# Row sums of an attention kernel: block transposes on VectorE instead of a transpose on TensorE, and a later turn for the last pair's first half

## The chip, the cores and the metric

The kernel runs on one core of one Trainium2 chip. The metric is the device time of one execution in microseconds; lower is better. The engines are called PE (TensorE; PEld is its weight load), DVE (VectorE), ACT (ScalarE), POOL (GpSimd) and SP (SyncE, which here only issues DMAs).

## The reference

Two encoder layers over 1024 tokens of width 1024, in float32. Layer 0 mixes with neighbourhood attention (mixer A), layer 1 with grouped-query attention (mixer B); both have 16 query heads of 64 dims, a softmax, and a gate. Cut to what matters here:

```python
sc = jnp.einsum('bkgqd,bksd->bkgqs', qb, k).astype(jnp.float32) * scale
pr = jax.nn.softmax(sc, axis=-1).astype(v.dtype)
o  = jnp.einsum('bkgqs,bksd->bkgqd', pr, v)
...
return (o * jax.nn.silu(gate)) @ w_out
```

After each mixer come a residual add, a second gated addition (per-layer embedding) and, at the end, one RMS norm.

## The kernel before

**Staging.** Mixer A, a dense stage, mixer B, a second dense stage. Matmuls work on float32 split in a high and a low part, so most products take three matmuls (L300 is the one line through which all of them go).

**Attention.** For each head and query tile: S (scores, with a row minimum `mn` by VectorE), E (exponential by ScalarE, with row sums `rs`), T (P transposed by PE into PSUM, then split by ScalarE into `PTh` and by VectorE into `PTl`), AV (PTh and PTl times V, into the PSUM tile `o`, four query tiles side by side). In mixer A all transposes, P's and others, draw on a PSUM pool of two buffers named `t`; in mixer B the pool of `o` has one buffer.

**The end of a head.** When the AV of half a head's queries is complete, `head_end` puts down what has to follow. Two heads (a pair) and one half of the queries (`hf`) share the tiles `Y` (outputs, 64 rows of each head), `rb` and `r8` (128 x 8: inverse row sums of four query tiles of the two heads). `evac` (L478) copies one half of `o` to Y, `join` (L441) adds the other half, which frees `o`; `norm` (L468) takes the reciprocal of the row sums. The outputs lie with queries along the free dimension, the inverse sums with queries along the partitions, so the sums have to be turned:

- For pairs 0 to 6, `rows` transposes `r8` on PE into PSUM (L445), ScalarE copies the 8 rows out (L447), SP stores them to DRAM as `rD` (L449), and two loads on SP bring them back to `rb`, each row of 512 values broadcast to 64 partitions (L451).
- For pair 7 `spread` (L455) copies the sums out along the free dimension and `across` (L461) transposes four 128 x 128 tiles on PE. For `hf` 0 ScalarE copies the result to `rb` (L464), for `hf` 1 it is used from PSUM.

`fin` then multiplies Y by the gate and by `rb` on POOL (L512, L513), and later ScalarE and VectorE split it (L509, L510) and SP stores it. `fin_last` does the same for pair 7 on VectorE; it calls `across` itself if that has not come yet.

**The order.** Every engine runs its instructions in the order in which the code emits them, and that order is written by hand. A list of attention items (one S, E, T or AV each) is mixed with dense items (projections and gates) by their costs. After each attention item comes one pulse. `post.add(n, f)` calls f n pulses later; `later` counts query tiles in the same way. So `evac` comes `DO` pulses after the last AV, `join` one pulse after it, `rows` `DD[layer][0]` pulses after the reciprocal, the store and the loads `DD[layer][1]` pulses after `rows`, and `across` `DT` pulses after the reciprocal. In mixer B two AV items lie nine or more pulses apart. Where one engine has to wait, all that stands behind in its queue waits too.

There are 28 groups that go through `rows`: 7 pairs, 2 halves, 2 layers. Four go through `across`.

Of the kernel before, what the change touches and what calls it, by code (L numbers as in the profile page):

```python
# [11 lines left out]
F32 = mybir.dt.float32  # L12
# [3 lines left out]
AF = mybir.ActivationFunctionType  # L16
# [16 lines left out]
DG, DR, DQ, DY, NP = 1, 2, 2, 1, 8  # L33
KT, KN = 2, 4
DO = (2, 3)
DD = ((3, 2), (5, 2))
DT = 2
FIN = (4, 4)
HOLD = 2
DP = 1  # L40
# [112 lines left out]
def trunk(ctx, tc, x, wts, rpb, gains, hgains, mask, rope, out):  # L153
    nc = tc.nc
    sync, act, dve, pool, pe = nc.sync, nc.scalar, nc.vector, nc.gpsimd, nc.tensor
# [7 lines left out]
    ident = glob.tile([128, 128], F32, name="ident")  # L163
# [133 lines left out]
    post = Later()  # L297
# [131 lines left out]
    def head_end(sb, h, hf, rs, Ops, ylive, layer, gg, talloc):  # L429
        pair = h // 2  # L430
        b = (h % 2) * 64
        if h % 2 == 0:
            Y = sb.tile([128, 512], F32, name="Y", bufs=2)
            rb = sb.tile([128, 512], F32, name="rb", bufs=2)
            r8 = sb.tile([128, 8], F32, name="r8", bufs=4)
            ylive[pair, hf] = (Y, rb, r8, {})
        Y, rb, r8, tail = ylive[pair, hf]
        yh = Y[b:b + 64]

        def join():  # L440
            dve.scalar_tensor_tensor(yh, Ops[0:64], 0.5, yh, op0=ALU.mult, op1=ALU.add)  # L441

        def rows():
            ps = talloc()
            pe.transpose(ps[0:8, 0], r8, ident)  # L445
            r8T = sb.tile([8, 128], F32, name="r8T", bufs=2)
            act.activation(r8T, ps[0:8, 0], AF.Copy)  # L447
            rD = dram.tile([8, 128], F32, name="rD", bufs=4)
            post.add(DD[layer][1], lambda: sync.dma_start(rD, r8T))  # L449
            for i in range(2):  # L450
                post.add(DD[layer][1], lambda i=i: sync.dma_start(  # L451
                    rb[64 * i:64 * i + 64], bass.AP(tensor=rD.tensor, offset=rD.offset + 512 * i, ap=[[0, 64], [1, 512]])))

        def spread():
            dve.tensor_copy(rb.rearrange("p (t j c) -> p t j c", t=4, j=2),  # L455
                            r8.rearrange("p (j t) -> p t j", j=2)[:, :, :, None].to_broadcast([128, 4, 2, 64]))

        def across():
            ps = talloc()
            for t in range(4):  # L460
                pe.transpose(ps[:, t], rb[:, t * 128:(t + 1) * 128], ident)  # L461
            ps = ps.rearrange("p t c -> p (t c)")
            if hf == 0:
                act.activation(rb, ps, AF.Copy)  # L464
            tail["rb"] = rb if hf == 0 else ps

        def norm():
            dve.reciprocal(r8[:, 4 * (h % 2):4 * (h % 2) + 4], rs)  # L468
            if h % 2 == 0:
                return  # L470
            if pair < 7:
                post.add(DD[layer][0], rows)
            else:
                spread()
                post.add(DT, across)

        def evac():
            act.activation(yh, Ops[64:128], AF.Copy, scale=0.5)  # L478
            post.add(DY, join)
            norm()  # L480
        if h == NH - 1 and hf == 1:
            evac()
        else:
            post.add(DO[layer], evac)
        if h % 2 == 0:
            return None
        G = gg.pop((pair, hf))
        del ylive[pair, hf]

        def fin_last():  # L490
            dve.tensor_tensor(Y, Y, G, ALU.mult)
            if "rb" not in tail:
                post.l = [e for e in post.l if e[1] is not across]
                across()
            dve.tensor_tensor(Y, Y, tail["rb"], ALU.mult)
            y3 = Y.rearrange("p (t c) -> p t c", t=4)
            ts = slice(4 * hf, 4 * hf + 4)
            act.activation(HTh[:, ts, 7, :], y3, AF.Copy)
            dve.tensor_tensor(HTl[:, ts, 7, :], y3, HTh[:, ts, 7, :], ALU.subtract)

        def fin():
            yhi, ylo = rb.bitcast(F32R), Y.bitcast(F32R)

            def store(c, src):
                sync.dma_start(yD[layer][c][4 * hf:4 * hf + 4, :, pair, :].rearrange("t p c -> p t c"),
                               src.rearrange("p (t c) -> p t c", t=4))

            def split():
                act.activation(yhi, Y, AF.Copy)  # L509
                dve.tensor_tensor(ylo, Y, yhi, ALU.subtract)  # L510
                post.add(2, lambda: (store(0, rb), store(1, Y)))
            pool.tensor_tensor(Y, Y, G, ALU.mult)  # L512
            pool.tensor_tensor(Y, Y, rb, ALU.mult)  # L513
            post.add(YS[layer], split)
        return fin_last if pair == 7 else fin
# [793 lines left out]
```

## Time and profile before

| | |
|---|---|
| median of 3 runs | 1598.41 us (1597.3 to 1602.05) |
| the profiled execution | 1600.45 us, of which 1598.7 is the span of the program |
| PE busy | 96% of the span |
| DVE, ACT, POOL busy | 64%, 55%, 17% |
| mean granted PE clock | 0.993 |
| mixer A's attention | about 85 to 540 us |
| mixer B's attention | about 800 to 1405 us |

Rows of the timeline read: start in us, duration in us, engine, line, operation, out<-in, and in brackets how long the engine was idle before it and what it waited for. The end of a matmul is modelled, since matmuls are pipelined; the distance from one start to the next is the measured thing. A row of the waits reads: who waited, for whom, us in total, how often, the longest.

### The profile page before, as it was taken

The page shows a single profiled execution, that of the slowest core. Times are in us where ns is not written, and L with a number is a line of the kernel's source. Part 1 is how long each engine was busy: PE and PEld are TensorE (multiplying, and loading weights), DVE is VectorE, ACT ScalarE, POOL GpSimd, SP SyncE. Part 2 cuts the span into 40 slices and gives each one's busy share as a digit, 9 for nine tenths or more (in the row PEclk, how much of TensorE's full clock was granted, in tenths as well). Part 3 has the DMA queues.
Part 4 walks back from the last instruction along what each step waited for, and adds up shares of the span by engine and source line. Part 5 has one row for each costly group of instructions (what it writes and reads, how often), then busy time and mean ns, then how long its engine had stood idle before and what let it go on. Part 6 is the DMA issues. An engine that isn't in the chain of part 4 may idle for free.

```text
span 1598.7 us, 24250 instructions
## 1 busy us (share of the span) xinstructions
PE 1534.7 (96%) x9076; PEld 1332.9 (83%) x9076; DVE 1021.4 (64%) x2034; ACT 878.4 (55%) x1772; POOL 268.3 (17%) x372
## 2 busy tenths in 40 slices
PE   6999999999999999999999999999999999899997
PEld 5888988988988788889888889888888788678886
DVE  6566576476476436567867777677676777524636
ACT  6565465465466423333466766766666777522422
POOL 2102102112112010000312222434122100000023
PEclk9999999999999999999999999999999999899999
DMA  8211222122124961232200111111101213551113
GB/s 268 77 52 56 66 69 73 52 78 76 39 92 120 351 209 40 93 126 98 69 19 21 47 48 45 55 33 55 41 21 40 73 47 123 201 197 53 67 56 129
DMA packets 88518, 138.85 MB, mean 87 GB/s; under 512 B 15344, under 2 KB 54608, under 8 KB 88400
## 3 DMA queue, kind: packets, MB, share of 16 engines
q1 hardware_dynamic: 83792, 122.62, 23.6%
q10 hardware_dynamic: 4608, 14.68, 2.6%
q8 instruction: 71, 1.16, 0.3%
q14 instruction: 47, 0.39, 0.1%
HBM read 104.65 MB, written 36.15 MB: 88 GB/s over the span
## 4 chain that ended last, share of the span: by engine, by line
PE 38%; DVE 7%; ACT 6%; issue 2%; DMA 0%; POOL 0%; ACTq 0%; DVEq 0%
PE d L300 21%; PE o L300 6%; PE s L300 5%; PE t L1064 5%; DVE PTl L1067 2%; ACT P L1054 1%; DVE mn L1048 1%; ACT PTh L1066 1%; DVE QS L1031 1%; DVE wl L216 1%; ACT wh L215 1%; PE t L425 1%; ACT QS L1030 0%; ACT rb L509 0%; ACT th L1026 0%
## 5 line engine op out<-in xcount | busy, mean ns | idle before, releaser
L300 PE MATMUL d<-wh,HTh 128*128 128x256 f32 (+1 forms) x1096 | 372.7, 340 | 4.7 <-ACT HTh L426 2.1
L300 PE MATMUL d<-wh,HTl 128*128 128x256 f32 (+1 forms) x1096 | 365.7, 334 | 1.5 <-DVE HTl L427 1.5
L300 PE MATMUL d<-wl,HTh 128*128 128x256 f32 (+1 forms) x1096 | 365.2, 333 | 0.0
L1067 DVE TENSOR_TENSOR PTl<-t,PTh 128x512 fp32r<-128x512 f32 x256 | 164.7, 685 | 110.2 <-ACT PTh L1066 109.3
L300 PEld LDWEIGHTS d<-wh,HTh 128*128 128x128 f32 x1096 | 207.8, 190 | 28.1 <-ACT HTh L426 2.7
L300 PEld LDWEIGHTS d<-wh,HTl 128*128 128x128 f32 x1096 | 207.7, 190 | 24.0 <-DVE HTl L427 2.3
L300 PEld LDWEIGHTS d<-wl,HTh 128*128 128x128 f32 x1096 | 208.1, 190 | 21.4
L300 PE MATMUL d<-HTh,wh 128*128 128x512 f32 x504 | 206.9, 411 | 0.0
L300 PE MATMUL d<-HTh,wl 128*128 128x512 f32 x504 | 198.3, 393 | 0.0
L300 PE MATMUL d<-HTl,wh 128*128 128x512 f32 x504 | 197.9, 393 | 0.0
L300 PE MATMUL o<-PTh,V 128*128 128x256 f32 (+2 forms) x672 | 174.6, 290 | 5.0 <-ACT r8T L447 4.1
L300 PE MATMUL o<-PTl,V 128*128 128x256 f32 (+2 forms) x672 | 174.6, 290 | 2.0 <-DVE PTl L1067 1.5
L1066 ACT ACTIVATE PTh<-t 128x512 fp32r<-128x512 f32 x256 | 140.1, 593 | 63.0 <-PE t L1064 62.4
L1054 ACT ACTIVATE P<-s,mn 128x1024 f32<-128x1024 f32 x128 | 142.4, 1113 | 48.8 <-DVE mn L1048 48.3
L1048 DVE TENSOR_REDUCE mn<-s 128x1 f32<-128x1024 f32 x128 | 155.2, 1213 | 11.8 <-PE s L300 11.4
L1064 PE MATMUL t<-ident,P 128*128 128x128 f32 x1024 | 138.2, 276 | 7.9 <-DVE PTl L1067 7.0
L300 PE MATMUL s<-KA,QS 128*128 128x512 f32 (+2 forms) x384 | 134.6, 405 | 10.0 <-ACT PTh L1066 5.6
L216 DVE TENSOR_TENSOR wl<-wstage,wh 128x1024 fp32r<-128x1024 f32 x89 | 114.0, 1286 | 39.3 <-ACT wh L215 38.7
L300 PEld LDWEIGHTS o<-PTh,V 128*128 128x128 f32 x672 | 128.7, 192 | 11.6 <-ACT r8T L447 6.2
L1064 PEld LDWEIGHTS t<-ident,P 128*128 128x128 f32 x1024 | 115.6, 141 | 23.9 <-DVE PTl L1067 18.6
L300 PEld LDWEIGHTS o<-PTl,V 128*128 128x128 f32 x672 | 129.0, 192 | 7.1 <-DVE PTl L1067 2.8
L300 PE MATMUL s<-KB,QS 128*128 128x512 f32 (+2 forms) x384 | 122.3, 372 | 0.0
(183 smaller groups left out, 2453.8 us busy)
## 6 DMA issues: line engine op xcount, KB each, us to landing
wstage<-in_wts SPq DMA_DIRECT2D x92, 512.0 KB, 3.5
X<-in_x SPq DMA_DIRECT2D x16, 512.0 KB, 7.5
pp<-ppD SPq DMA_DIRECT2D x32, 256.0 KB, 3.1
rb<-rD SPq DMA_DIRECT2D x56, 128.0 KB, 2.9
ppD<-th SPq DMA_DIRECT2D x24, 256.0 KB, 2.0
xD<-X SPq DMA_DIRECT2D x8, 512.0 KB
X<-xD SPq DMA_DIRECT2D x8, 512.0 KB, 7.6
yD0h<-rb SPq DMA_DIRECT2D x14, 256.0 KB, 2.2
```

Source lines behind the costliest of these rows:

```text
L215: act.activation(hi, s, AF.Copy)
L216: self.rest = lambda: dve.tensor_tensor(lo, s, hi, ALU.subtract)
L300: pe.matmul(ps, a, b, start=first, stop=last, skip_group_check=True)
L425: pe.transpose(ps[:, k], xn[:, (4 * c + k) * 128:(4 * c + k + 1) * 128], ident)
L1031: post.add(DQ, lambda qs=qs, own=own, oth=oth: dve.tensor_tensor(qs[oth], raw[own], qs[own], ALU.subtract))
L1048: dve.tensor_reduce(mn, ps, axis=AX.X, op=ALU.min)
L1054: act.activation(p, ps, AF.Exp, bias=mn, scale=-1.0, accum_out=RS[h, hf][:, t:t + 1])
L1064: pe.transpose(ps[:, i], p[:, k * 128:(k + 1) * 128], ident)
L1066: act.activation(PTh[:, ks, c], ps, AF.Copy)
L1067: dve.tensor_tensor(PTl[:, ks, c], ps, PTh[:, ks, c], ALU.subtract)
```

## The change

`rows` no longer uses PE, PSUM or ScalarE. One VectorE instruction transposes `r8`, read four times over to make 32 columns, in blocks of 32 x 32: of 32 partitions each, the eight columns become rows 32b to 32b + 7 of `r8T`, with 32 values each. The four pieces are then stored by four DMAs of 8 rows of 128 B; the two broadcast loads stay. In mixer B (`DD[1]`) `rows` comes three pulses after the reciprocal instead of five, as in mixer A. `DT` becomes a pair: `across` comes five pulses after the reciprocal for `hf` 0, in both layers, and two as before for `hf` 1.

```diff
-DD = ((3, 2), (5, 2))
-DT = 2
+DD = ((3, 2), (3, 2))
+DT = (5, 2)
...
         def rows():
-            ps = talloc()
-            pe.transpose(ps[0:8, 0], r8, ident)
-            r8T = sb.tile([8, 128], F32, name="r8T", bufs=2)
-            act.activation(r8T, ps[0:8, 0], AF.Copy)
+            r8T = sb.tile([128, 32], F32, name="r8T", bufs=2)
+            dve.transpose(r8T.rearrange("p (a c) -> p a c", a=4), r8[:, None].to_broadcast([128, 4, 8]))
             rD = dram.tile([8, 128], F32, name="rD", bufs=4)
-            post.add(DD[layer][1], lambda: sync.dma_start(rD, r8T))
+            for b in range(4):
+                post.add(DD[layer][1], lambda b=b: sync.dma_start(rD[:, 32 * b:32 * b + 32], r8T[32 * b:32 * b + 8]))
...
                 spread()
-                post.add(DT, across)
+                post.add(DT[hf], across)
```

## The prediction

> **What bounds the kernel now.** I read the page first, then the busy time by stage, then the waits of PE, then the timeline at the places that the diff touches.
>
> ```profile
> span 1598.7 us, 24250 instructions
> PE 1534.7 (96%) x9076; PEld 1332.9 (83%) x9076; DVE 1021.4 (64%) x2034; ACT 878.4 (55%) x1772; POOL 268.3 (17%) x372
> PEclk9999999999999999999999999999999999899999
> ```
> ```profile
> 100.00:515.00 415.00, 412.28 (x2392) 361.04 (x2391) 262.05 (x574) 242.77 (x548) 73.81 (x93) 1.00 0.23 70
> 840.00:1352.00 512.00, 490.99 (x3326) 437.23 (x3325) 372.14 (x594) 355.65 (x667) 124.67 (x200) 1.00 0.15 46
> ```
> (Columns: window, length, then busy us of PE, PE's weight loads, VectorE, ScalarE and POOL with counts, clock, DMA share, GB/s.) PE is the bound: 99% busy in mixer A's stage, 96% in mixer B's. In B it idles 21.0 us of 512, while VectorE (73%) and ScalarE (69%) have a quarter free. So PE work that goes is worth its time, and an idle of PE is worth its time unless the next wait takes it up. Which waits are they?
>
> ```profile
> PE t L1064 <- DVE PTl L1067: 7.0, 12, 1.4
> PE o L300 <- ACT r8T L447: 4.1, 5, 1.2
> PE o L445 <- DVE Y L441: 3.0, 6, 1.0
> ```
> (Total us, times, longest.) Two of the three belong to the step that the diff rewrites: in B the tile `o` has one buffer, so the transpose at L445 waits for the join (L441) to free it, and the next AV matmul waits until ScalarE has copied the 8 rows out.
>
> **Row sums: what is removed.** Each of the 28 groups loses one PE transpose and one ScalarE copy. Cheap place (A), then dear place (B):
>
> ```profile
> 119.54 0.27 PE L445 MATMUL t<-ident,r 128*8 128x128 f32 x1
> 119.57 0.48 PE L300 MATMUL d<-HTh,wh 128*128 128x512 f32 x1
> 119.88 0.39 PE L300 MATMUL d<-HTl,wh 128*128 128x512 f32 x1
> 120.11 0.40 PE L300 MATMUL d<-HTh,wl 128*128 128x512 f32 x1
> ...
> 842.00 0.27 PE L445 MATMUL o<-ident,r 128*8 128x128 f32 x1
> 842.01 1.10 ACT L1054 ACTIVATE P<-s,mn 128x1024 f32<-128x1024 f32 x1
> 843.10 0.25 ACT L447 ACTIVATE r8T<-o 8x128 f32<-8x128 f32 x1
> 843.40 0.39 PE L300 MATMUL o<-PTh,V 128*128 128x256 f32 x1 [1.13 <-ACT r8T L447]
> ```
> At the cheap place the next matmul starts 0.03 us after the transpose, but takes 0.31 us to the one after it where 0.23 is usual: 0.11 us in all. At the dear place the small copy stands behind a 1.10 us exponential in ScalarE's queue, and PE loses 1.40 us from start to start: the idle 1.13 and the transpose's own 0.27.
>
> - Five dear places: 4.1 + 5 x 0.27 = 5.4 us.
> - Six places where the transpose waits for the join: 3.0 us. At those that I looked up, gate or q matmuls stand between it and the next AV, so the join has time to end behind them.
> - The other 17 or so at 0.11 us, with the small part in the six: 23 x 0.11 = 2.5 us.
>
> Gross 10.9 us. The 2.5 is plain PE time and I keep it. Of the 8.4 in waits PE comes early to its next wait: late next are VectorE's PTl before the P transposes (7.0 us in 12 waits already). With a quarter of VectorE and ScalarE free I keep three quarters, 6.3 us; the ends are 0 and 8.4.
>
> **Row sums: what is added.** 28 VectorE block transposes of 128x32. None is in the trace; the nearest rows are the reciprocal of 4 columns below (0.17 us) and the 512-column join (0.69, quoted further down), and I take 0.2 because 32 columns are nearest to the first. They wait only for the reciprocal in front of them on the same engine (and for a store two groups back). Queued behind each are a PTl or a row minimum, on which PE waits at times: 14 in B, 2.8 us, of which I charge a quarter, 0.7; ends 0 and 14 x 0.69 = 9.7. In A's stage VectorE has 153 us free and PE's slack hides it.
>
> ```profile
> L468 DVE RECIPROCAL r<-rs x64: 167/170/176, 85.3 to 1397.1; 128x4 f32<-128x4 f32 x64
> L449 SPq DMA_DIRECT2D rD<-r8T x28: 288/290/679, 113.3 to 1331.9; - x28
> 113.25 0.35 SPq L449 DMA_DIRECT2D rD<-r8T  x1
> 114.50 1.14 SPq L451 DMA_DIRECT2D rb<-rD  x2
> 196.62 0.33 SPq L449 DMA_DIRECT2D rD<-r8T  x1
> 200.27 1.09 SPq L451 DMA_DIRECT2D rb<-rD  x2
> ```
> ```profile
> 203.87 1.30 POOL L513 TENSOR_TENSOR Y<-Y,rb 128x512 f32<-128x512 f32 x1 [8.75 <-DMA rb<-rD]
> 206.68 0.62 ACT L509 ACTIVATE rb<-Y 128x512 fp32r<-128x512 f32 x1
> ```
> One store of eight 512 B rows becomes four of eight 128 B rows: 3 x 0.29 = 0.87 us more on SP's queue for each group, and the two broadcast loads behind them wait for all four. The trace has no 128 B store: store to load is 1.25 us in the quiet case and 3.65 beside weight traffic. If the four overlap, rb comes 0.87 us later; if they land one after another, 3 x 3.65 = 11 us later at the second place. I take 0.87, since one store holds SP for 0.29 us only. What covers it: POOL's multiply ends at 205.17 and ScalarE takes its result at 206.68, so 1.5 us of cover, and I count three such places in A (pairs that end beside a V projection). Elsewhere there is more. So: nothing. SP's later issues (weights, tables) move by the same 0.87 us; no row of PE's waits names a DMA.
>
> Beside those rows: the Trainium skill, "DMA: Bandwidth & Descriptors", Specifications, says that below 512 B the DMA engine does a read-modify-write. If that doubled the quiet 1.25 us, rb would come 0.87 + 1.25 = 2.1 us later, 0.6 beyond the cover at three places, an estimated 1.9 us off the gain. No row here shows such a write.
>
> In B the step also goes from five pulses after the reciprocal to three: the block transpose, four stores and two loads move ahead of what two pulses issue on VectorE and SP. rb is then no later than before; its reader POOL comes well after. Zero.
>
> **Last pair, first half.** `across` transposes rb back on PE three pulses later. In B:
>
> ```profile
> 1358.45 1.04 PE L1064 MATMUL t<-ident,P 128*128 128x128 f32 x8
> 1359.79 0.63 PE L300 MATMUL s<-KB,QS 128*128 128x512 f32 x2
> 1362.95 0.69 DVE L441 SCALAR_TENSOR_TENSOR Y<-o,Y 64x512 f32<-64x512 f32 x1
> 1363.78 1.09 PE L461 MATMUL o<-ident,rb 128*128 128x128 f32 x4 [3.36 <-DVE Y L441]
> 1364.90 0.60 ACT L464 ACTIVATE rb<-o 128x512 f32<-128x512 f32 x1 [3.88 <-PE o L461]
> 1367.23 1.91 PE L1064 MATMUL t<-ident,P 128*128 128x128 f32 x8
> 1370.10 0.28 PE L300 MATMUL o<-PTh,V 128*128 128x256 f32 x1
> ```
> ```profile
> 1362.00:1364.00 2.00, 0.22 (x1) 0.25 (x2) 1.60 (x2) 0.00 (x0) 0.00 (x0) 0.66 1.02 402
> 1364.00:1366.00 2.00, 2.00 (x8) 1.71 (x8) 0.00 (x0) 0.60 (x1) 0.00 (x0) 0.50 0.35 142
> 1366.00:1368.00 2.00, 2.00 (x8) 1.60 (x7) 0.00 (x0) 0.49 (x1) 0.00 (x0) 0.50 0.00 0
> 1368.00:1370.00 2.00, 2.00 (x10) 1.82 (x9) 0.83 (x2) 1.48 (x4) 0.00 (x0) 0.64 0.35 131
> 1395.00:1400.00 5.00, 4.23 (x21) 3.79 (x20) 1.80 (x4) 1.08 (x2) 0.00 (x0) 0.68 0.02 5
> ```
> PE stands 3.36 us for the join, and meanwhile its clock falls to half: the eight transposes take 1.91 us where they took 1.04. The lost clock from 1364 to 1370 is 1.0 + 1.0 + 0.7 = 2.7 us. Three pulses later by the order of the code is after the next step's T and E and before its S and AV. So after S (until 1360.4) PE runs six `d` matmuls (6 x 0.23, to 1361.8) and T (1.0, to 1362.8), waits for the join (1363.64; start 1363.78: 1.0 us of the wait stays), transposes rb (to 1364.35) and does S (four matmuls, 0.9, to 1365.3); ScalarE's copy of 0.60, late now, holds the AV matmul until about 1365.6. Before it began at 1370.10: 4.5 us gained, with ends 0 (the wait just moves) and 3.4 + 2.7 = 6.1. In A `across` draws on a pool with two buffers and hardly waits: zero.
>
> **The sum.** 6.3 + 2.5 + 4.5 - 0.7 = 12.6 us of a profiled span of 1598.7 (its run took 1600.45, with 1.75 around the span; the median of the runs, 1598.41, is 2.04 below that run). The gain goes against the median: 1598.4 - 12.6 = 1585.8.
>
> **The rivals.**
>
> *The clock falls all the same.* It also fell with no long idle:
>
> ```profile
> 1392.20 1.03 PE L1064 MATMUL t<-ident,P 128*128 128x128 f32 x8
> 1394.27 1.25 PE L1064 MATMUL t<-ident,P 128*128 128x128 f32 x8 [1.04 <-DVE PTl L1067]
> 1395.95 0.38 PE L300 MATMUL o<-PTh,V 128*128 128x256 f32 x1 [0.43 <-ACT PTh L1066]
> ```
> From 1392.2 to 1395.95 PE ran transposes only, with 1.04 and 0.43 us idle, and from 1395 to 1400 the clock was 0.68. In the new order T, the rest of the wait and `across` leave PE without a matmul of its own from 1361.8 to 1364.35, 2.5 us. That is less than 3.75, but enough to make this open. It costs the 2.7 us: 1588.5. The Trainium skill, "TensorE: Matmul & The Clock Gate", Part 4, says that transposes don't count as PE-busy for the clock; these rows agree with it.
>
> *The waits come back.* If PE in B is held by VectorE and ScalarE, who carry much of the chain between the places, PE reaches the next PTl sooner and waits there: 2.5 stays, and half of the 4.5 or so: 4.5 in all, 1593.9. For it: the 12 waits on PTl. Against: the waits that go come from the latency of one buffer, not from a full engine, and both engines have a quarter free.
>
> *Slower: the four stores land one after another under weight traffic.* At the three places of A rb would come 11 us later, 9.5 beyond the cover; ScalarE, in order, stands for POOL, and PE behind it: 28.4 us lost, 1614. It decides from a delay of (12.6 + 4.8) / 3 + 1.5 = 7.3 us at each of them, over 2.4 us for each extra store. Against: SP's short issue, and sixteen DMA engines that are a quarter busy there (share 0.23).
>
> **How the numbers follow.** Forecast 0.52; better than it, with all waits kept and the whole 6.1 (10.9 + 6.1 = 17.0, 1581.4) 0.08; clock falls 0.18; waits come back 0.15; slower 0.07. A measurement can tell about 0.3%, 4.8 us: faster is below 1593.6. The third is on that line, I give 0.05 of it to faster. So faster 0.83, within 0.3% 0.10, slower 0.07. Range 1580 to 1596: from just past all kept to just past the waits that come back.
>
> **What would show it.** Right: no L445 and no wait on r8T on PE; 28 VectorE transposes near 0.2 us; 112 stores; PE's idle in B down by 6 us or more; the wait at `across` at about 1 us and digit 35 of the clock row at 9. Wrong: PTl or PTh waits of PE up by as much as the others fell (the second rival), transposes over 0.5 us, ScalarE waiting for POOL at L509 beyond today's sites (the third), or a new digit 8 in the clock row.

## The result and the profile after

The changed kernel takes 1585.26 us (median, 1583.41 to 1588.54), the kernel before, beside it on the same chip, 1598.28: 13.0 us less, a ratio of 0.992 (95% interval 0.9905 to 0.9934). In a second set on another chip it was 1583.06 against 1598.39, ratio 0.9905 (0.9889 to 0.992). The profiled execution took 1586.45, its span 1584.7. 1585.8 had been forecast.

From the page after:

```profile
span 1584.7 us, 24269 instructions
PE 1527.3 (96%) x9048; PEld 1331.9 (84%) x9048; DVE 1025.0 (65%) x2062; ACT 872.8 (55%) x1744; POOL 266.8 (17%) x372
PEclk9999999999999999999999999999999999999999
```

28 PE instructions and 28 of ScalarE fewer, 28 of VectorE more, and the 8 in the clock row is gone. (A digit stands for a slice of 40 us, so a short fall can hide behind a 9; the last section shows one.) Mixer B's stage by engine (columns as before), then PE's waits over the whole span, by what ended them (us in all, how many, the longest):

```profile
840.00:1352.00 512.00, 497.09 (x3371) 446.41 (x3371) 381.04 (x616) 359.52 (x666) 124.79 (x200) 1.00 0.17 51
```
```profile
PE t L1063 <- DVE PTl L1066: 7.0, 12, 1.4
PE o L300 <- DVE PTl L1066: 2.5, 7, 0.9
PE o L460 <- DVE Y L441: 1.0, 1, 1.0
```

PE idles 14.9 us there instead of 21.0. The waits on `r8T` and before the row transpose are gone; the waits before the P transposes, named as late next, stand at 7.0 in 12 as before, and AV's wait for PTl rose by 1.0 us in all, from this row of the profile before:

```profile
PE o L300 <- DVE PTl L1067: 1.5, 4, 0.9
```

The line numbers have moved by one.

To see where the time went, take one instruction in both traces: ScalarE's exponential of the same query tile, early in B, before the last pair, and after it. First before:

```profile
1355.07 1.13 ACT L1054 ACTIVATE P<-s,mn 128x1024 f32<-128x1024 f32 x1
1374.15 1.11 ACT L1054 ACTIVATE P<-s,mn 128x1024 f32<-128x1024 f32 x1
```

and after (the first of these belongs to the row at 842.01 of the prediction):

```profile
842.84 1.10 ACT L1053 ACTIVATE P<-s,mn 128x1024 f32<-128x1024 f32 x1
1346.57 1.13 ACT L1053 ACTIVATE P<-s,mn 128x1024 f32<-128x1024 f32 x1
1360.75 1.11 ACT L1053 ACTIVATE P<-s,mn 128x1024 f32<-128x1024 f32 x1
```

At the start of B the changed kernel is 0.83 us behind, before the last pair 8.50 us ahead, behind it 13.40. So the row sums gave 9.3 us in B, the last pair 4.9, and mixer A with what precedes B lost 0.8. I call this the stage reading and use it below, since whole times scatter by several microseconds; it always goes against the one profile of before.

Between the first two of these points, in B, the windows split the 9.3 us (before, then after):

```profile
842.01:1355.07 513.06, 492.05 (x3329) 438.14 (x3328) 372.53 (x594) 355.89 (x669) 124.45 (x200) 1.00 0.16 48
842.84:1346.57 503.73, 488.82 (x3315) 438.82 (x3314) 374.40 (x608) 352.71 (x654) 124.57 (x200) 1.00 0.16 48
```

PE's idle fell from 21.0 to 14.9 us, which is 6.1 of the 9.3: 7.1 us of waits went (4.1 and 3.0), and about 1.0 came back at AV. The other 3.2 us are PE's busy time, the 14 transposes that are gone. (The ends of matmuls are modelled, so the sum of the two is surer than the split.)

### The profile page after: what moved, and what is told of

It is laid out like the page before. It is cut to its first block, busy times and chain, and to the rows that moved or that the text cites. A ratio compares the mean times of both kernels' runs of the same rounds, so it can differ in the third digit from the quotient of the medians.

```text
span 1584.7 us, 24269 instructions
## 1 busy us (share of the span) xinstructions
PE 1527.3 (96%) x9048; PEld 1331.9 (84%) x9048; DVE 1025.0 (65%) x2062; ACT 872.8 (55%) x1744; POOL 266.8 (17%) x372
## 4 chain that ended last, share of the span: by engine, by line
PE 39%; DVE 6%; ACT 5%; issue 2%; POOL 0%; ACTq 0%; DVEq 0%
PE d L300 21%; PE o L300 6%; PE s L300 6%; PE t L1063 5%; DVE PTl L1066 2%; ACT PTh L1065 1%; ACT P L1053 1%; DVE mn L1047 1%; DVE QS L1030 1%; PE t L425 1%; ACT QS L1029 1%; ACT wh L215 0%; ACT rb L508 0%; DVE wl L216 0%; ACT th L1025 0%
## 5 line engine op out<-in xcount | busy, mean ns | idle before, releaser
L1047 DVE TENSOR_REDUCE mn<-s 128x1 f32<-128x1024 f32 x128 | 154.9, 1210 | 10.8 <-PE s L300 10.4
```

The costliest lines, as they stand in the source:

```text
L1047: dve.tensor_reduce(mn, ps, axis=AX.X, op=ALU.min)
```

## The experiments

**The later turn alone.** The kernel before with

```diff
-DT = 2
+DT = (5, 2)
...
-                post.add(DT, across)
+                post.add(DT[hf], across)
```

> The kernel before with the later turn of the last pair's first half alone (DT = (5, 2)); row sums still go through PE. My theory (the wait on the join and the fall of the clock behind it are the whole of that part, and the two parts are independent): PE's wait at the four transposes of rb falls from 3.4 to about 1.0 us, the clock row keeps its nines there, and the time falls by about 5 us, to 1593. Rival (the two parts need each other: with the row transposes left in, PE comes to that place otherwise loaded): under 2 us of gain.

1594.52 against 1598.67, ratio 0.9967 (0.9954 to 0.998): 4.2 us. PE's wait at the four transposes is 1.0 us, the clock row has nines, and the stage reading gives 4.9 us at that place. The later turn works without the new row sums. Mixer A, where nothing is changed up to its last pair, ended 1.4 us later than in the profile before: one execution against another says nothing about 1 us in A.

**Rows alone**, twice: the changed kernel with `DT = (2, 2)`.

> The changed kernel with DT = (2, 2): row sums by VectorE alone. My theory: the PE waits on the row copy and on the join before the row transpose are gone, about 9 us gained in mixer B and about 1 us lost in mixer A, so about 8 us faster than before, 1590; at the last pair PE's wait of 3.4 us and the half clock for some 6 us are back. Rival (waits come back elsewhere once the clock fall is there): under 5 us.

1584.89, ratio 0.991 (0.9894 to 0.9927): faster than expected, and no slower than the changed kernel had been in its own set. That would leave nothing for the later turn, so both ran again, side by side.

> The changed kernel again, beside the next three on the same chip. The first runs put rows alone (DT = (2, 2)) at 1584.9 and the changed kernel at 1585.3, in different sets of runs. Theory (the later turn saves the 2.4 us of PE's idle in every execution, and 2.4 us more where the clock would have fallen there): the changed kernel is 2.4 to 4 us faster than rows alone beside it, near 1583 when rows alone is at 1586. Rival (the later turn gives nothing once the rows are off PE): the two agree within 1 us.

> Rows by VectorE with DT = (2, 2), again. Theory as for the changed kernel beside it: 2.4 to 4 us slower than it, at about 1586. In the profile PE waits 3.4 us for the join at the four transposes of rb; whether the clock falls behind it differs between executions, and where it does the place costs 2.4 us more. Rival: same time as the changed kernel.

1583.06 for the changed kernel (1582.58 to 1583.16) and 1588.5 for rows alone (1584.35 to 1592.1): beside each other the later turn is worth 5.4 us, more than both expectations. But rows alone is the same kernel in both sets, and its medians lie 3.6 us apart; all ten executions of it have a median of 1586.4, all eight of the changed kernel 1583.3, so whole times put the later turn at about 3 us and no closer. One part of the spread shows at the last pair in the profile of rows alone, in its timeline and then by stretches:

```profile
1351.37 0.68 DVE L441 SCALAR_TENSOR_TENSOR Y<-o,Y 64x512 f32<-64x512 f32 x1
1352.19 0.63 PE L460 MATMUL o<-ident,rb 128*128 128x128 f32 x4 [3.35 <-DVE Y L441]
1354.05 1.04 PE L1063 MATMUL t<-ident,P 128*128 128x128 f32 x8
```
```profile
1350.00:1352.00 2.00, 0.00 (x0) 0.00 (x0) 1.97 (x3) 0.00 (x0) 0.00 (x0) 1.00 0.99 342
1352.00:1354.00 2.00, 1.80 (x10) 1.58 (x11) 0.05 (x1) 0.60 (x1) 0.00 (x0) 1.00 0.58 234
```

The same wait of 3.35 us is there, but in this execution the clock did not fall behind it: the eight transposes take 1.04 us, not 1.91. The other profile of rows alone shows the same, 3.36 us of wait and a clock of 1.00 behind it. The stage reading makes this place 2.4 us shorter in both than in the profile of before, where the clock did fall. The six timed executions run from 1584.35 us at a mean clock of 0.998, which is the profiled one, to 1592.1 at 0.994. One fall of 2.4 us doesn't make these 7.75; where the clock fell in the slower ones no profile shows.

**Rows on VectorE in mixer B only**; mixer A's go through PE and ScalarE as before.

```diff
+            if layer == 1:
+                r8T = sb.tile([128, 32], F32, name="r8T", bufs=2)
...
+            else:
+                ps = talloc()
+                pe.transpose(ps[0:8, 0], r8, ident)
+                r8T = sb.tile([8, 128], F32, name="r8T8", bufs=2)
+                act.activation(r8T, ps[0:8, 0], AF.Copy)
...
```

> The changed kernel with mixer A's row sums on PE and ScalarE as before, mixer B's on VectorE. My theory (in A the VectorE transpose buys PE 1.5 us, but rb comes later and the phase of VectorE against POOL shifts, and A's stage ended 1.0 us later than before): A's stage ends as it did before, and the whole is 1 us faster than the changed kernel, about 1584. Rival (A's 1.0 us is scatter of one execution and the VectorE way gains its 1.5 us there): A's stage ends later than in the changed kernel and the whole is 0.5 to 1.5 us slower, 1586 to 1587.

1583.09 (1582.05 to 1584.94), ratio 0.9899 (0.9885 to 0.9914). Inconclusive on A: it agrees with the second set of the changed kernel (1583.06), not with the first. Against the profile before, A ended +0.4 us here, and between +0.7 and +1.4 in three more kernels with the old way in A; with VectorE's way it ended between -1.4 and +1.2 in eight executions. So what the change gives A, or takes from it, is not told apart from the scatter, and the loss that I had read from one profile lies within it. For B the stage reading says 9.2 us again.

**The PE transpose with a pool of two buffers.** The kernel before with the later turn; in B the row transpose writes to the pool of the P transposes (`ralloc` takes from that pool in mixer B, and is `talloc` in mixer A):

```diff
-            ps = talloc()
+            ps = ralloc()
             pe.transpose(ps[0:8, 0], r8, ident)
```

> The kernel before with DT = (5, 2), and in mixer B the row transpose on PE writes to the PSUM pool of two buffers that the P transposes use, not to the single buffer of the AV output. PE transpose, ScalarE copy and one store stay. Theory 1 (the gain in B comes from the single buffer: the transpose waiting for the join, and AV waiting for the copy): most of it comes back without VectorE, 6 to 8 us beyond the 5 of DT, 1586 to 1588. Theory 2 (it comes from taking the copy off ScalarE's queue and the transpose off PE, whatever the buffer): the P transposes now wait for the ScalarE copy instead, and it gains under 3 us beyond DT, 1590 to 1593.

1595.24, ratio 0.9981 (0.9972 to 0.999): no gain over the later turn alone, and in B it is 2.0 us slower than the kernel before. Theory 1 is refuted as far as this other pool goes; theory 2's wait was not quite the one either. From its waits:

```profile
PE t L445 <- DVE PTl L1067: 9.0, 9, 1.9
```

The transpose now waits for VectorE to free a buffer of P, 9.0 us in place of the 3.0 + 4.1, and those 1.9 us more are about what B lost. In both pools that were tried the 8 rows have somebody to wait for; a buffer of their own was not tried.

**The turn of the rows**, on VectorE and on PE. The changed kernel with `DD[1] = (5, 2)`, and the kernel before with `DT = (5, 2)` and `DD[1] = (3, 2)`:

> The changed kernel with DD[1] = (5, 2): mixer B's VectorE transposes at the old, later turn. My theory (the gain in B is the PE transpose and its two waits; the earlier turn is worth nothing, since rb is read much later): B's stage gains the same 9 us against the kernel before, and the time is that of the changed kernel within 1 us. Rival (the earlier turn carries part of it, by keeping the transpose out of the DVE work ahead of the next P transposes): 2 us or more slower than the changed kernel.

> The kernel before with DT = (5, 2) and DD[1] = (3, 2): mixer B's row sums still on PE, but at the earlier turn of the changed kernel. My theory (on PE the transpose waits for the join to free the one buffer, so an earlier turn meets the join less often finished): PE's wait for the join before the row transposes rises from 3.0 us in 6 places to 10 us or more, and the time from 1594.5 (DT alone) to about 1600. Rival (the earlier turn itself is a gain, whatever engine turns the rows): 1592 or less.

On VectorE at the old turn: 1583.29, ratio 0.9908 (0.9895 to 0.9921), the changed kernel's time, with 10.5 us gained in B. On PE at the earlier turn: 1602.95, ratio 1.0024 (1.0012 to 1.0037), 8.4 us more than the later turn alone had in another set; by the stage reading B is 7.3 us slower than before.

```profile
PE o L445 <- DVE Y L441: 15.6, 13, 2.1
```

The wait for the join rose from 3.0 us in 6 places to 15.6 in 13, while AV's wait for the copy (4.1 us) is gone: 8.5 us more in all. The turn matters here for PE, which has something to wait for, and not for VectorE; both theories held, with the second kernel 3 us slower than I had put it.

**Which half of the wait.** The changed kernel at the old turn, with the PE transpose put back in B beside VectorE's; its result is not used, so AV waits for nobody:

```diff
+            if layer == 1:
+                pe.transpose(talloc()[0:8, 0], r8, ident)
```

> The changed kernel with DD[1] = (5, 2), and in mixer B the old PE transpose into the AV output's one buffer put back at its old place beside the VectorE one. Nobody reads it, so AV doesn't wait for ScalarE; what returns is the transpose and its wait for the join. Theory: the 3.0 us in six waits for the join and about 0.1 us for each of 14 transposes return, 4 to 5 us slower than the changed kernel (1583), at 1587 to 1588; the other half of the gain in B, AV's wait for the copy (4.1 us of idle in 5 places), stays away. Rival (the gain hangs on the copy alone): under 1.5 us slower.

1589.16 (1588.88 to 1590.68), ratio 0.9939 (0.9924 to 0.9954): 5.9 us over the same kernel without it in another set.

```profile
PE o L447 <- DVE Y L441: 3.0, 6, 1.0
```

The 3.0 us in six are back to the digit, and so are about 3.1 us of PE's busy time (491.9 us between the same two points, 488.8 in the changed kernel). B's gain fell from the 9.3 of the changed kernel (10.5 without the transpose at this turn) to 3.1 us: the transposes and their wait for the join cost 6.2 to 7.4. The 3.1 that stay belong to the copy, AV's wait for it and the relief of ScalarE together; no run parts these two.

**The price of the added instruction.** Every block transpose done twice:

```diff
+            r8X = sb.tile([128, 32], F32, name="r8X", bufs=2)
+            dve.transpose(r8X.rearrange("p (a c) -> p a c", a=4), r8[:, None].to_broadcast([128, 4, 8]))
```

> The changed kernel with every VectorE block transpose done twice (the second into a tile that nobody reads). It prices the added instruction. The step of my sum charged a quarter of its time in B, 0.7 us in all. Theory (hidden, since VectorE has a quarter free): 0 to 1 us slower than the changed kernel (1583 to 1584 by the last set). Rival (VectorE carries the chain in B, so each one is paid in full): 28 x 0.2 = 5.6 us slower, 1588.5.

1583.7, ratio 0.9905 (0.989 to 0.9921), and 9.2 us gained in B. The second transposes (0.17 us each) are hidden; the 0.7 us that I had charged was too much.

**The copy's own time on ScalarE.** A copy of `r8T` into a tile that nobody reads:

```diff
+            r8C = sb.tile([128, 32], F32, name="r8C", bufs=2)
+            act.activation(r8C, r8T, AF.Copy)
```

> The changed kernel with a ScalarE copy of r8T into a tile that nobody reads, 28 copies at the place of the old ones. It prices the copy's own time on ScalarE, apart from what waited for it. Theory (the copy's own time is hidden; what cost was AV waiting for it): 0 to 1.5 us slower than the changed kernel. Rival (the relief of ScalarE is part of the gain): 4 us or more slower.

1600.53, ratio 1.0016 (1.0004 to 1.0028): 17 us slower than the changed kernel, beyond both. It doesn't price what it was made for. From its waits and timeline:

```profile
ACT r8C L447 <- DVE r8T L445: 44.2, 24, 5.8
```
```profile
192.77 3.45 DVE L216 TENSOR_TENSOR wl<-wstage,wh 128x1024 fp32r<-128x1024 f32 x2
196.15 0.55 DVE L672 TENSOR_TENSOR PTl<-t,PTh 128x384 fp32r<-128x384 f32 x1
196.62 0.20 DVE L445 STREAM_TRANSPOSE r8T<-r 128x32 f32<-128x32 f32 x1
196.84 0.23 ACT L447 ACTIVATE r8C<-r8T 128x32 f32<-128x32 f32 x1 [2.52 <-DVE r8T L445]
196.98 0.60 ACT L660 ACTIVATE sp<-sp,mn 128x384 f32<-128x384 f32 x1
```

28 copies of 0.23 us are 6.4 us of work, but ScalarE stands 44.2 us for VectorE, whose transposes come behind two weight splits and more; the exponential behind the copy waits too. By the stage reading it lost about 13 us in mixer A, and 1 of the 9 in B. In A, PE's wait for that exponential rose to 12.1 us (5.8 in the changed kernel), and the clock fell at three places, to 0.76 from 200 to 205 us and to 0.66 from 325 to 330 and from 450 to 455: about 5 us more, an estimate from these stretches of 5 us. What the copy's time alone is worth stays open. What the run does show is that the block transpose's late place in VectorE's queue does no harm where only stores on SP follow it, and costs 17 us where a ScalarE instruction does.

**One pulse later still.** The changed kernel with `DT = (6, 2)`:

> The changed kernel with DT = (6, 2): across one pulse later still, behind the S of the next but one step. My theory (1.0 us of the wait for the join is left, and S, 0.9 us, then covers it, but the copy of rb by ScalarE now holds the next AV matmul longer): PE's wait at the four transposes falls below 0.2 us, a wait of AV on the copy of rb of 0.5 to 0.8 us comes, so 0 to 0.5 us faster: the same within the scatter. Rival (the copy is not what holds AV): 1.0 us faster in that stage.

1584.47, ratio 0.9914 (0.99 to 0.9929): no difference that these runs can tell, and the stage reading gives 4.9 us at that place as in the changed kernel. The wait for the join is gone and AV waits for the copy of rb:

```profile
PE o L300 <- ACT rb L463: 0.8, 1, 0.8
```

No version that I ran is clearly faster than the changed kernel.

## Why the prediction was right, step by step

**The total** (12.6 us forecast, 13.0 and 15.3 measured) came from the right places, with sizes that were off in both directions. That the errors nearly cancelled is luck.

**Row sums, removed: right in mechanism, too low in B.** I had a gross of 8.4 us, of which 7.1 were waits and 1.35 the transposes at the dear places, kept three quarters of it, and put 0.11 us for each remaining transpose. The stage reading gives 9.2 to 10.5 us in B in eight executions. Two terms were too small. The share kept: in the profile after, 6.1 of the 7.1 us of waits stayed away, since the wait before the P transposes stood at 7.0 us and only AV's wait for PTl grew, by 1.0. And the transposes: the sum had 5 x 0.27 + 9 x 0.11 = 2.3 us for the 14 in B, and 3.2 us of busy time went, 0.23 for each; 0.11 was read at one place in A. The other way, the 1.5 us that the sum kept for A's 14 transposes is not shown by these runs. By halves, the sum's own terms are 3.0 + 2.3 = 5.3 us for the transposes with their wait, where 6.2 to 7.4 were measured, and 4.1 for the copy, where 3.1 were.

**Row sums, added: right.** The block transposes take what was taken for them:

```profile
L445 DVE STREAM_TRANSPOSE r8T<-r x28: 195/202/208, 111.7 to 1322.3; 128x32 f32<-128x32 f32 x28
```

0.202 us against 0.2. The charge of 0.7 us was not needed, as the doubled transposes show.

**The four stores: right, and the slower rival is refuted.** Quiet place and the place beside weight traffic, after:

```profile
111.98 1.34 SPq L448 DMA_DIRECT2D rD<-r8T  x4
114.30 1.14 SPq L450 DMA_DIRECT2D rb<-rD  x2
196.73 1.31 SPq L448 DMA_DIRECT2D rD<-r8T  x4
200.24 1.09 SPq L450 DMA_DIRECT2D rb<-rD  x2
```

First store to load is 2.32 us where one store had 1.25, so 1.07 more (0.87 had been put), and 3.51 us beside the weights where one store had 3.65. The four overlap. The sign that I had named for this rival, ScalarE waiting longer for POOL's multiply, stood at 10.4 us in 3 places before, 12.1 in 4 after, and 10.1 in 3 in the second profile of the changed kernel: no clear rise. The doubling that I had estimated from the Trainium skill's rule on transfers under 512 B ("DMA: Bandwidth & Descriptors", Specifications) would have made the quiet case 1.25 + 2.1 = 3.4 us; the measured 2.32 shows no such price for eight rows of 128 B, at most the 0.2 us beyond the 0.87 of issue.

**The last pair: right by its own timeline.** I had put the wait at 1.0 us and AV 4.5 us earlier (by stages this place gave 4.9); PE's timeline of the changed kernel:

```profile
1355.19 0.66 PE L460 MATMUL o<-ident,rb 128*128 128x128 f32 x4 [1.01 <-DVE Y L441]
1355.60 0.71 PE L300 MATMUL s<-KA,QS 128*128 128x512 f32 x2
1356.62 0.37 PE L300 MATMUL o<-PTh,V 128*128 128x256 f32 x1
```

The same place by stretches, the granted clock third from the right:

```profile
1354.00:1356.00 2.00, 0.99 (x8) 0.76 (x7) 1.94 (x4) 2.00 (x5) 0.00 (x0) 1.00 0.96 380
```

The wait is 1.01 us, AV starts 13.48 us before its time at 1370.10, of which 8.5 were gained earlier: 5.0. The rival in which the clock falls all the same did not happen: 1.00 through the place, here and in the ten other profiles of kernels with the later turn.

**Where it was wrong: the profiled execution was not a typical one.** Of the 4.9 us, 2.4 are the clock's fall. It is in the profile of before (1600.45 us), which I had noted to lie 2.04 us over the median, and I still set the whole gain against the median. Rows alone show that the fall at that place is not in every execution. So the later turn is worth about 2.5 us where the clock would have held and 4.9 where it would have fallen, and the step "the gain goes against the median" should have taken a part of that off. With 9.3 us in B the sum would then be 11.8 to 14.2, beside 13.0 and 15.3 in the two sets. The part that was counted too high here made up for the part that was too low in B.

## What to carry to other kernels

A tiny step on a busy engine can cost many times its length when it takes a shared buffer: count what waits for the buffer and what the step waits for, and look for an engine on which it has no one to wait for and nothing in order behind it that waits. In this kernel, 6.1 of 7.1 us of waits taken off the bound engine stayed away, with a quarter free on the engines that feed it; a wait put onto ScalarE, 28 copies of 0.23 us, cost 17 us through what stood behind it. Before a term is read from a profile, see whether that execution stands beside the median or apart from it, and why.

## What the runs showed of the hardware

The granted clock of PE falls at the same code in some executions and not in others. A PE idle of 3.36 us ended in 0.50 of the clock in the profile of before; in both profiles of rows alone, an idle of 3.36 and 3.35 us ended at 1.00. One kernel shows it too. The changed kernel was profiled twice. Here is, in both, the later stretch that the prediction quotes from 1392.20 on (two times eight transposes with short waits), first by the second eight transposes:

```profile
1380.83 1.25 PE L1063 MATMUL t<-ident,P 128*128 128x128 f32 x8 [1.04 <-DVE PTl L1066]
1379.07 1.25 PE L1063 MATMUL t<-ident,P 128*128 128x128 f32 x8 [1.04 <-DVE PTl L1066]
```

and by stretches, the first profile and then the second:

```profile
1380.00:1385.00 5.00, 3.68 (x20) 3.06 (x21) 3.09 (x6) 1.74 (x4) 0.00 (x0) 0.84 0.14 52
1385.00:1390.00 5.00, 4.70 (x22) 3.81 (x21) 2.06 (x3) 1.19 (x2) 0.00 (x0) 0.82 0.11 41
```
```profile
1380.00:1385.00 5.00, 4.49 (x28) 3.46 (x27) 2.84 (x6) 1.88 (x4) 0.00 (x0) 1.00 0.00 0
1385.00:1390.00 5.00, 4.20 (x19) 2.98 (x18) 1.81 (x4) 2.39 (x4) 0.00 (x0) 1.00 0.29 108
```

The same transposes and the same wait of 1.04 us are followed by a fall in the first and by none in the second. So the fall from 1395 to 1400 that the prediction read off the profile before doesn't show by itself that transposes let the clock fall.

The mean clock goes with the time of one kernel: of 44 executions of the kernel before beside the experiments, ten at a mean clock of 0.997 took 1595.6 to 1597.6 us, seven at 0.993 took 1599.3 to 1602.7. Part of what looks like scatter is how often the clock fell. Whether a change that takes long waits off PE narrows the scatter is not shown: the changed kernel's second set lies within 0.6 us, its first within 5.1. What decides between a fall and none, the length being the same, these runs don't show.
